# A decoder trunk in fp32: V and gate of four retention heads as two Strassen pairs woven into the memory and rotary passes

## The chip, the cores and the metric

The kernel runs on one core of one Trainium2 chip. The metric is device time in microseconds (us) of one execution. TensorE is PE in the profile (its weight loads are PEld), VectorE is DVE, ScalarE is ACT, GpSimd is POOL, SyncE is SP. PE, DVE, ACT, POOL and SP each work through their own queue in the order in which it was written when the kernel was compiled; a semaphore holds an instruction back until what it reads is there and what it overwrites is free.

## The reference, cut to what matters

256 tokens of width 2048 go through one layer A, a shared K/V projection, and one layer B. The part that is changed lies in layer A:

```python
h = rmsnorm(x, g)
q, k, v, gate_r, mq, gate_m = split_cols(h @ w_in, [1024, 1024, 2048, 2048, 1024, 1024])
q = rotary(q.reshape(B, S, 8, 128)); k = rotary(k.reshape(B, S, 8, 128)) * 128 ** -0.5
o = retention(q, k, v.reshape(B, S, 8, 256))          # 8 heads, chunks of 128 tokens
o = o * lax.rsqrt(jnp.mean(o * o, axis=-1, keepdims=True) + EPS)
o_ret = o.reshape(B, S, 2048) * jax.nn.silu(gate_r)
o_mem = memory_branch(mq, gate_m, mem_n, w_mem_kv)    # 4 heads of 256 over 256 memory tokens
return x + jnp.concatenate([o_ret, o_mem], axis=-1) @ w_out
```

`memory_branch` makes its keys and values as `mem_n @ w_mem_kv`, takes a softmax, and multiplies by a SiLU gate. After layer A, `shared_kv` projects the normed x to K and V of three groups of heads, and layer B uses them.

## The kernel before

Everything is fp32 in and out. A factor is split into a high part (a cast to fp32r, by ACT) and a low part (the difference, by DVE), and a product takes three matmuls: high with high, high with low, low with high. `split(hi, lo, src)` (L96 to L98) is these two instructions. A weight block is 128x1024: it comes by DMA into a `raw` tile (6 buffers), is split into `wh` and `wl` (5 buffers each), and PE consumes it. All weights are used once, so PE, ACT and DVE each have work for every block.

There are three forms of product:

- A **column pass** (`dense_cols`, L306) makes 512 output columns, transposed, in two halves. In each half it goes through 16 row groups of the weights and 2 column tiles, and for each it issues one matmul of 512 columns (L315, high and low part of x side by side) and one of 256 (L317): a pair. `cols_plain2`, `gate_cols` and `rotary` use it.
- A **row pass** (`dense`, L431) makes 256 tokens by 512 columns: 96 matmuls of 512 columns (L440 to L442). V and gate of the retention heads are made so.
- A **Strassen pair** (`strassen`, L343) makes two 512-column blocks at once with 7 products instead of 8. Each of its 4 depth steps loads 3 weight blocks, DVE makes sums and differences of them (L361), and 7 products of 6 matmuls each follow (L371 to L373). It needs differences of x as well (`combine`, L329, eight of them with their splits). It is a generator that is advanced a product at a time.

The order is fixed when the kernel is compiled. Small work (norms, splits of x, attention) is held in generators in `pending`; `step()` inside a pass advances one. A Strassen pair stands in `woven`; `weave(n)` in a column pass advances it n products, (2, 2, 1, 0) after the four parts of a half and 3 after its eviction. Splits and weight sums of a woven pair are put ahead with a priority, so the ACT and DVE queues have them earlier than PE's order would.

PSUM has three accumulators, acc0 to acc2, taken in turn, and two smaller tiles, att. While a pair is woven it holds two of the three (L345). SBUF has 30 tiles of 128x1024 named `big`, which hold x, its splits, results and attention operands. `spill` (L778) writes such a tile to DRAM and `fetch` (L784) reads it back, both on POOL's queue.

The stages of layer A, by the numbers of the profile: memory keys (`w_mk`) 5 to 56 us, memory values (`w_mv`) 56 to 101 us, then for each of two pairs of memory heads the queries and the gate (`w_ac`, L839 and L840), then for each of two groups of four heads rotary q and k (L844, L845) and for each pair of heads V and gate as row passes (L848, L849). Memory attention and retention are `pending` work that later passes step through (L841, L850). Retention ends in a power on POOL (L655). The out-projection, memory keys and values of layer B, and the K/V projection follow; the last, from 719 to 1203 us, weaves six Strassen pairs into column passes (L905 to L914). At the start x is read as `xs`, a `SplitCols`: ACT multiplies by the norm's gain and casts, DVE multiplies and subtracts (L220, L221). `Scaled` (L755), used behind layer A, has DVE scale a copy first and then split it.

## Time and profile before

| | us |
|---|---|
| median of 3 runs | 1902.02 |
| lowest and highest of them | 1897.88, 1902.39 |
| the profiled execution | 1899.93 |
| its span | 1898.2 |
| PE busy in it | 1875.5 |
| DVE busy in it | 1317.7 |
| ACT busy in it | 985.8 |

The span is the time from the first to the last instruction of the profiled execution; the execution's own time is 1.7 us longer. Busy times are sums over one engine. A row of waits gives the waiting engine and line, the engine and line it waited for, the total, the count and the longest. The lines are those of the kernel before; in the kernel after, the same code stands one or a few lines further down.

### The profile page before, as it was taken

To read this page: it belongs to the slowest core of one execution; us is meant where nothing else is said; L and a number is where in the kernel's file an instruction comes from. 1 tells how busy PE (TensorE), PEld (TensorE's weight loads), DVE (VectorE), ACT (ScalarE), POOL (GpSimd) and SP (SyncE) were. 2 spreads that over 40 slices of the span, in tenths; PEclk is the share of its full clock that TensorE was granted. 3 is DMA by queue.
4 is the path that set the end of the run, shared out by engine and by line. 5 is a ranking of instruction groups with operands and counts; after the bars stand their busy time and mean duration, and the time that the engine had idled before them with its cause. 6 is when DMAs were issued, how large, how long until landed. Compare 5 with 4: busy or idle time off the path is not lost.

```text
span 1898.2 us, 25963 instructions
## 1 busy us (share of the span) xinstructions
PE 1875.5 (99%) x9988; PEld 1604.6 (85%) x9988; DVE 1317.7 (69%) x1571; ACT 985.8 (52%) x1288; POOL 47.5 (3%) x88
## 2 busy tenths in 40 slices
PE   8999999999999999999999999999999999999997
PEld 7888888888888888888888888788889898888886
DVE  7766765665564757899999999866657475656643
ACT  6554445444454645555655556554545454545543
POOL 1000000000000000000000000000000000000000
PEclk9999999999999999999999999999999999999999
DMA  9654565565676666575766667666655556566462
GB/s 304 234 167 157 162 202 180 168 202 184 215 253 208 196 213 212 201 251 192 244 211 222 240 203 256 233 222 210 202 187 181 187 160 218 165 207 220 151 199 100
DMA packets 112588, 385.25 MB, mean 203 GB/s; under 512 B 12385, under 2 KB 18577, under 8 KB 112465
## 3 DMA queue, kind: packets, MB, share of 16 engines
q1 hardware_dynamic: 102784, 349.22, 56.5%
q0 software_dynamic: 9536, 34.37, 5.0%
q8 instruction: 78, 1.28, 0.3%
q14 instruction: 46, 0.37, 0.1%
q10 hardware_dynamic: 144, 0.01, 0.0%
HBM read 364.68 MB, written 18.87 MB: 202 GB/s over the span
## 4 chain that ended last, share of the span: by engine, by line
PE 93%; DVE 2%; issue 2%; ACT 1%; DMA 1%; SPq 0%; POOL 0%; ACTq 0%; POOLq 0%; DVEq 0%
PE acc L315 33%; PE acc L317 17%; PE acc L440 9%; PE acc L441 9%; PE acc L442 9%; PE acc L371 4%; PE acc L372 4%; PE acc L373 4%; DVE wl L98 1%; PE att L102 1%; PE att L103 1%; PE att L101 1%; PE acc L298 1%; ACT wh L97 1%; PE att L714 1%
## 5 line engine op out<-in xcount | busy, mean ns | idle before, releaser
L98 DVE TENSOR_TENSOR wl<-raw,wh 128x1024 fp32r<-128x1024 f32 (+1 forms) x642 | 769.3, 1209 | 461.8 <-ACT wh L97 459.9
L97 ACT CAST wh<-raw 128x1024 fp32r<-128x1024 f32 (+1 forms) x642 | 660.4, 1040 | 673.8 <-PE acc L315 263.6
L315 PE MATMUL acc<-big,wh 128*128 128x512 f32 x2752 | 983.5, 400 | 5.6 <-DVE big L221 2.4
L317 PE MATMUL acc<-big,wl 128*128 128x256 f32 x2752 | 771.3, 280 | 0.8 <-DVE wl L98 0.8
L315 PEld LDWEIGHTS acc<-big,wh 128*128 128x128 f32 x2752 | 517.8, 188 | 127.7 <-DVE big L470 3.1
L317 PEld LDWEIGHTS acc<-big,wl 128*128 128x128 f32 x2752 | 520.2, 189 | 5.0 <-DVE wl L98 1.1
L440 PE MATMUL acc<-wh,big 128*128 128x512 f32 x744 | 291.6, 392 | 0.0
L441 PE MATMUL acc<-wl,big 128*128 128x512 f32 x744 | 289.8, 390 | 0.0
L442 PE MATMUL acc<-wh,big 128*128 128x512 f32 x744 | 289.8, 390 | 0.0
L442 PEld LDWEIGHTS acc<-wh,big 128*128 128x128 f32 x744 | 139.7, 188 | 29.1
L440 PEld LDWEIGHTS acc<-wh,big 128*128 128x128 f32 x744 | 139.8, 188 | 28.2
L441 PEld LDWEIGHTS acc<-wl,big 128*128 128x128 f32 x744 | 139.8, 188 | 27.8
L371 PE MATMUL acc<-wh,big 128*128 128x512 f32 x336 | 133.2, 397 | 1.2 <-ACT wh L97 1.0
L372 PE MATMUL acc<-wl,big 128*128 128x512 f32 x336 | 131.7, 392 | 0.5 <-DVE wl L98 0.5
L373 PE MATMUL acc<-wh,big 128*128 128x512 f32 x336 | 131.6, 392 | 0.0
L97 ACT CAST wh<-big 128x1024 fp32r<-128x1024 f32 x72 | 75.5, 1049 | 72.5 <-DVE big L361 57.7
L98 DVE TENSOR_TENSOR wl<-big,wh 128x1024 fp32r<-128x1024 f32 x72 | 87.8, 1220 | 19.3 <-ACT wh L97 19.1
L371 PEld LDWEIGHTS acc<-wh,big 128*128 128x128 f32 x336 | 63.1, 188 | 17.1 <-ACT wh L97 1.7
L373 PEld LDWEIGHTS acc<-wh,big 128*128 128x128 f32 x336 | 63.1, 188 | 14.8
L372 PEld LDWEIGHTS acc<-wl,big 128*128 128x128 f32 x336 | 63.2, 188 | 11.8 <-DVE wl L98 1.0
L361 DVE TENSOR_TENSOR big<-big,raw 128x1024 f32<-128x1024 f32 x48 | 58.5, 1219 | 0.3
L98 DVE TENSOR_TENSOR big<-big 128x512 fp32r<-128x512 f32 (+1 forms) x54 | 43.4, 823 | 4.6 <-ACT big L97 3.2
(230 smaller groups left out, 1264.5 us busy)
## 6 DMA issues: line engine op xcount, KB each, us to landing
raw<-in_w_b_dram SPq DMA_DIRECT2D x160, 512.0 KB, 3.5
raw<-in_w_kc_dram SPq DMA_DIRECT2D x96, 512.0 KB, 4.4
raw<-in_w_vs_dram SPq DMA_DIRECT2D x96, 512.0 KB, 4.5
raw<-in_w_ac_dram SPq DMA_DIRECT2D x64, 512.0 KB, 3.5
raw<-in_w_ar_dram SPq DMA_DIRECT2D x64, 512.0 KB, 3.9
raw<-in_w_oa_dram SPq DMA_DIRECT2D x48, 512.0 KB, 3.5
raw<-in_w_ob_dram SPq DMA_DIRECT2D x48, 512.0 KB, 3.5
raw<-in_w_mv_dram SPq DMA_DIRECT2D x32, 512.0 KB, 3.5
```

Source lines behind the costliest of these rows:

```text
L97: act.copy(hi, src)
L98: dve.tensor_tensor(lo, src, hi.bitcast(F32), ALU.subtract)
L101: pe.matmul(o, lhsT=ah, rhs=bh, start=first, stop=False, skip_group_check=True)
L315: pe.matmul(ps[:, ct].rearrange("p h s -> p (h s)"), lhsT=wh[:, cs], rhs=xhl(part, a), start=first, stop=False, skip_group_check=True)
L317: pe.matmul(ps[:, ct, 0, :], lhsT=wl[:, cs], rhs=xh(part, a), start=False, stop=last, skip_group_check=True)
L361: f(*args)
L371: pe.matmul(ps, lhsT=h, rhs=wh[:, cs], start=first, stop=False, skip_group_check=True)
L372: pe.matmul(ps, lhsT=h, rhs=wl[:, cs], start=False, stop=False, skip_group_check=True)
L373: pe.matmul(ps, lhsT=l, rhs=wh[:, cs], start=False, stop=last, skip_group_check=True)
L440: pe.matmul(ps[t], lhsT=xh(part, a)[:, ts], rhs=wh, start=first, stop=False)
L441: pe.matmul(ps[t], lhsT=xh(part, a)[:, ts], rhs=wl, start=False, stop=False)
L442: pe.matmul(ps[t], lhsT=xl(part, a)[:, ts], rhs=wh, start=False, stop=last)
```

## The change

Layer A's V and gate of heads 0 to 3, four row passes, become two Strassen pairs (`w_as`), each giving V and gate of one pair of heads. Their products are advanced from inside the gate pass of the first memory pair, the query and gate passes of the second, and the rotary q pass of the first head group, at (2, 1, 1, 0) and 3. `xs` becomes a `Scaled` that scales in place (`own`), since the pairs need x times the gain for their differences. Memory keys and values of layer A are written to DRAM when they are made and fetched by `mem_job` when their attention begins; V and gate of the pairs are written by `done_a` and fetched by `ret_job`. Memory attention now runs in the rotary passes of the first head group, retention of heads 0 to 3 in those of the second. The first half of the second memory-key block takes the accumulator acc2 by name. In layer B, `mem_job` fetches and splits memory keys and values behind the gate pass instead of inside the query pass.

```diff
+    rate, banks = [2, 1, 1, 0, 3], []
-    def dense_cols(xs, w, c, evict, g=None):
+    def dense_cols(xs, w, c, evict, g=None, name=None):
         for i in range(2):
-            ps = acc_tile()
+            ps = acc_tile(name if i == 0 else None)
...
-                weave((2, 2, 1, 0)[j])
+                weave(rate[j])
...
-                weave(3)
+                weave(rate[4])
...
-    def strassen(parts, comb, w, done, banks=[]):
+    def strassen(parts, comb, w, done):
...
-            self.raw[j] = big_tile()
+            self.raw[j] = self.src[j] if self.own else big_tile()
...
+    def mem_job(mk, mv, q, gt, nrm, c):
+        k = split_big(fetch(mk))
+        yield
+        v = split_big_rows(fetch(mv))
+        yield
+        yield from mem_attention(q, k, v, gt, nrm, mix.tile(4 + c))
+
+    def ret_job(m, qT, kT):
+        v, gt = va[m]
+        v = split_big_rows(fetch(v))
+        gt = rows(fetch(gt))
+        yield
+        yield from retention(2 * m, 2 * (m % 2), qT, kT, v, gt, n_x.hr, mix.tile(m))
+        yield from mix.halves(m)
...
-    xs = SplitCols(xt, GA)
+    xs = Scaled(GA, own=True)
...
-        mk_a.append(split_big(mk0))
+        mk_a.append(spill(flat(mk0)))
...
-            yield from xs.halves(i)
+            yield from xs.start(i)
...
-    mk1 = cols_scaled(None, ms, w_mk[0], 1)
+    mk1 = cols_scaled(None, ms, w_mk[0], 1, name="acc2")
...
-    mk_a.append(split_big(mk1))
+    mk_a.append(spill(flat(mk1)))
...
-    mv_a = [rows_scaled2(dense(ms, w_mv[0], c), n_m.r) for c in range(2)]
+    mv_a = [spill(rows_scaled(dense(ms, w_mv[0], c), n_m.r).rearrange("p t c -> p (t c)")) for c in range(2)]
...
+    def done_a(m):
+        def f(o1, o2):
+            for t in range(2):
+                act.activation(o1[:, t, :], o1[:, t, :], AF.Copy, scale=n_x.r[:, t:t + 1])
+            g = gate_rows([o2[:, t, :] for t in range(2)], n_x.hr)
+            va[m] = [spill(o.rearrange("p t c -> p (t c)")) for o in (o1, g)]
+        return f
+
+    pending.append(combine(xs.raw, combx))
+    mq, gm = [], []
     for c in range(2):
-        mq = cols_plain2(xs, w_ac, 4 + c)
-        gm = gate_cols(n_x.bh, xs, w_ac, 6 + c)
-        pending.append(mem_attention(mq, mk_a[c], mv_a[c], gm, n_x, mix.tile(4 + c)))
-        pending.append(mix.halves(4 + c))
+        mq.append(cols_plain2(xs, w_ac, 4 + c))
+        if c == 0:
+            drain()
+            for m in range(2):
+                woven.append(strassen(xs, combx, w_as[m], done_a(m)))
+        gm.append(gate_cols(n_x.bh, xs, w_ac, 6 + c))
     for hg in range(2):
-        qT = rotary(cosr, sinr, xs, w_ac, hg)
-        kT = rotary(cosr, sinr, xs, w_ac, 2 + hg)
-        for u in range(2):
-            m = 2 * hg + u
-            v = rows_scaled2(dense(xs, w_ar, m), n_x.r)
-            gt = gate_rows(dense(xs, w_ar, 4 + m), n_x.hr)
-            pending.append(retention(2 * m, 2 * u, qT, kT, v, gt, n_x.hr, mix.tile(m)))
-            pending.append(mix.halves(m))
+        pending.append(mem_job(mk_a[hg], mv_a[hg], mq[hg], gm[hg], n_x, hg) if hg == 0 else ret_job(0, qT, kT))
+        q_ = rotary(cosr, sinr, xs, w_ac, hg)
+        pending.append(mem_job(mk_a[1], mv_a[1], mq[1], gm[1], n_x, 1) if hg == 0 else ret_job(1, qT, kT))
+        qT, kT = q_, rotary(cosr, sinr, xs, w_ac, 2 + hg)
+        if hg == 0:
+            while woven:
+                weave()
+    banks.clear()
+    for u in range(2):
+        m = 2 + u
+        v = rows_scaled2(dense(xs, w_ar, u), n_x.r)
+        gt = gate_rows(dense(xs, w_ar, 2 + u), n_x.hr)
+        if u == 0:
+            pending.append(mix.halves(4))
+            pending.append(mix.halves(5))
+        pending.append(retention(2 * m, 2 * u, qT, kT, v, gt, n_x.hr, mix.tile(m)))
+        pending.append(mix.halves(m))
...
+                rate[:] = [2, 2, 1, 0, 3]
...
-        pending.append(split_kv(c))
         mq = cols_plain2(yb, w_b, 16 + c)
         drain()
         gm = gate_cols(None, yb, w_b, 18 + c)
-        pending.append(mem_attention(mq, mkb2[c], mvb2[c], gm, n_y, mix.tile(4 + c)))
+        pending.append(mem_job(mk_b[c], mv_b[c], mq, gm, n_y, c))
```

Three places in the order of the engines' instructions. The first is PE's queue at the end of the first memory-key block and the start of the second; acc0_378 and acc2_378 are the accumulator of the second block's first half, acc1_112 the last one of the first block, and att_561 the tile of the norm's sums. Before:

```order
L298 MATMUL acc1_112<-big_322,wh_347 128x512
L300 MATMUL acc1_112<-big_322,wl_348 128x256
L174 MATMUL att_561<-ones_83,sqsum_395 128x1 x2
L315 MATMUL acc0_378<-big_126,wh_381 128x512
L317 MATMUL acc0_378<-big_126,wl_382 128x256
```

After:

```order
L299 MATMUL acc1_112<-big_322,wh_347 128x512
L301 MATMUL acc1_112<-big_322,wl_348 128x256
L316 MATMUL acc2_378<-big_126,wh_381 128x512
L318 MATMUL acc2_378<-big_126,wl_382 128x256
L316 MATMUL acc2_378<-big_126,wh_381 128x512
```

The second block's first matmul goes to acc2 instead of acc0, and the norm's sums no longer stand ahead of it.

The second is DVE's queue from the norm of x on, where the first column pass of layer A begins. `nbh` and `rope_t` are norm factors; `wl<-raw,wh` is a split of a weight block. Before, `big<-big,gain` is the low part of x:

```order
L201 TENSOR_SCALAR nsd_x<-r_x 128x2
L98 TENSOR_TENSOR wl<-raw,wh 128x1024
L521 SCALAR_TENSOR_TENSOR big<-acc_779,r_m,big 128x512
L198 TENSOR_SCALAR nbh<-nb 128x256
L810 TENSOR_TENSOR rope_t<-rope_t,nb 128x256
L811 TENSOR_TENSOR rope_t<-rope_t,nb 128x256
L221 SCALAR_TENSOR_TENSOR big<-big,gain 128x256
L521 SCALAR_TENSOR_TENSOR big<-acc_779,r_m,big 128x512
L221 SCALAR_TENSOR_TENSOR big<-big,gain 128x256 x2
L98 TENSOR_TENSOR wl<-raw,wh 128x1024
L221 SCALAR_TENSOR_TENSOR big<-big,gain 128x256 x8
L98 TENSOR_TENSOR wl<-raw,wh 128x1024
```

After, `big<-big 128x2x256` is the low part of x, L337 a difference of x and `big<-sm,big` or `big<-p,big` the low part of one:

```order
L202 TENSOR_SCALAR nsd_x<-r_x 128x2
L99 TENSOR_TENSOR wl<-raw,wh 128x1024
L337 TENSOR_TENSOR p<-big 128x512
L337 TENSOR_TENSOR p<-big,sm 128x512
L199 TENSOR_SCALAR nbh<-nb 128x256
L832 TENSOR_TENSOR rope_t<-rope_t,nb 128x256
L833 TENSOR_TENSOR rope_t<-rope_t,nb 128x256
L99 TENSOR_TENSOR big<-big 128x2x256 x7
L99 TENSOR_TENSOR wl<-raw,wh 128x1024
L99 TENSOR_TENSOR big<-big 128x2x256
L99 TENSOR_TENSOR big<-sm,big 128x512
L99 TENSOR_TENSOR wl<-raw,wh 128x1024
```

The eight differences and their splits now stand in this stretch, and x is split in eight instructions instead of sixteen.

The third is ACT's queue where the second pair ends. Before, this stretch of layer A is the row passes: weight casts, then V (L520) and gate (L527) from the accumulator:

```order
L97 CAST wh<-raw 128x1024 x6
L520 ACTIVATE big<-acc_2398,r_x 128x512
L97 CAST wh<-raw 128x1024
L520 ACTIVATE big<-acc_2398,r_x 128x512
L97 CAST wh<-raw 128x1024 x6
L527 ACTIVATE big<-acc_2549,hr_x 128x512
```

After, L528 is the tanh of the pair's gate, L867 the scaling of its V, the last `big<-big 128x1024` the cast of the fetched memory V of the second pair of heads, and L583 the exponentials of its attention:

```order
L528 ACTIVATE big<-big,hr_x 128x512
L98 CAST big<-p 128x512
L98 CAST big<-big 128x1024
L867 ACTIVATE big<-big,r_x 128x512
L428 COPY big<-acc_1279 128x512
L98 CAST wh<-raw 128x1024
L867 ACTIVATE big<-big,r_x 128x512
L98 CAST wh<-raw 128x1024 x2
L98 CAST big<-big 128x1024
L583 ACTIVATE p,ls<-acc_2915,nm,sc_x 128x256 x2
```

POOL's queue at that place, before:

```order
L184 TENSOR_TENSOR r_m<-r_m,mhalf 128x2
L184 TENSOR_TENSOR r_x<-r_x,mhalf 128x2
L655 TENSOR_TENSOR cf<-cf,mhalf 128x2 x8
L781 DMA spill_4620<-big 128x1024
L781 DMA spill_4847<-big 128x1024
```

And after, where 610, 614, 772 and 970 are memory K and V, 1997, 1995, 2859 and 2857 V and gate of the pairs:

```order
L783 DMA spill_1997<-big 128x1024
L783 DMA spill_1995<-big 128x1024
L808 DMA big<-spill_610 128x1024
L808 DMA big<-spill_772 128x1024
L808 DMA big<-spill_614 128x1024
L783 DMA spill_2859<-big 128x1024
L783 DMA spill_2857<-big 128x1024
L808 DMA big<-spill_970 128x1024
L808 DMA big<-spill_1995 128x1024
L808 DMA big<-spill_1997 128x1024
L656 TENSOR_TENSOR cf<-cf,mhalf 128x2 x2
```

The fetch of memory V of the second pair of heads (970) stands behind the spills of the second Strassen pair, and retention's powers stand behind all of these.

## Rows read from the trace of the kernel before

**Rows 1.** Page, part 1: busy us, share of the span, instructions

```profile
PE 1875.5 (99%) x9988; PEld 1604.6 (85%) x9988; DVE 1317.7 (69%) x1571; ACT 985.8 (52%) x1288; POOL 47.5 (3%) x88
```

**Rows 2.** PE's waits, whole run: line, releaser: total us, times, longest

```profile
PE acc L315 <- DVE big L221: 2.4, 1, 2.4
PE acc L315 <- DVE big L470: 2.2, 2, 2.0
```

**Rows 3.** Windows: us, busy PE, PEld, DVE, ACT, POOL, PEclk, DMA share, GB/s

```profile
300.00:460.00 160.00, 160.00 (x826) 136.52 (x825) 103.95 (x129) 79.66 (x112) 4.14 (x6) 1.00 0.57 184
745.00:840.00 95.00, 95.00 (x479) 79.98 (x478) 88.00 (x84) 53.50 (x57) 2.67 (x5) 1.00 0.68 224
745.00:1200.00 455.00, 453.22 (x2267) 380.01 (x2266) 425.04 (x400) 259.40 (x280) 11.19 (x21) 1.00 0.67 225
1240.00:1320.00 80.00, 80.00 (x474) 70.27 (x473) 49.31 (x58) 40.73 (x53) 2.16 (x4) 1.00 0.62 206
```

**Rows 4.** Waits from 100 to 460 us, layer A

```profile
ACT wh L97 <- PE acc L442: 55.6, 38, 1.7
```

**Rows 5.** Waits from 745 to 1190 us, the K/V weave

```profile
ACT wh L97 <- DVE raw L361: 83.1, 21, 6.2
ACT wh L97 <- DVE big L361: 55.1, 21, 4.2
...
ACT wh L97 <- PE acc L373: 12.4, 18, 3.1
```

**Rows 6.** Timeline, PE, row pass: start us, us, instruction

```profile
70.01 0.39 PE L442 MATMUL acc<-wh,big 128*128 128x512 f32 x1
...
70.69 0.39 PE L442 MATMUL acc<-wh,big 128*128 128x512 f32 x1
```

**Rows 7.** Timeline, PE, K/V weave: Strassen matmuls, then column pairs

```profile
769.85 0.39 PE L371 MATMUL acc<-wh,big 128*128 128x512 f32 x1
...
770.53 0.39 PE L315 MATMUL acc<-big,wh 128*128 128x512 f32 x1
...
772.64 0.40 PE L315 MATMUL acc<-big,wh 128*128 128x512 f32 x1
```

**Rows 8.** Timeline, PE, start of the second memory-key block, [idle before <-releaser]

```profile
30.93 0.50 PE L174 MATMUL att<-ones,sqsum 128*128 128x1 f32 x4
33.43 0.50 PE L315 MATMUL acc<-big,wh 128*128 128x512 f32 x1 [2.00 <-DVE big L470]
```

**Rows 9.** Timeline, PE, memory attention: first and last of 12 matmuls in a row

```profile
155.00 0.28 PE L101 MATMUL att<-big 128*128 128x256 f32 x1
...
156.32 0.28 PE L103 MATMUL att<-big 128*128 128x256 f32 x1
```

**Rows 10.** Timeline, DVE, K/V weave, instructions back to back

```profile
765.79 1.22 DVE L98 TENSOR_TENSOR wl<-big,wh 128x1024 fp32r<-128x1024 f32 x1
766.93 4.73 DVE L98 TENSOR_TENSOR wl<-raw,wh 128x1024 fp32r<-128x1024 f32 x4
...
788.13 0.68 DVE L405 TENSOR_TENSOR big<-acc,p 128x512 f32<-128x512 f32 x1
788.73 0.68 DVE L406 TENSOR_TENSOR big<-acc,p 128x512 f32<-128x512 f32 x1
```

**Rows 11.** DVE by form, 745 to 1190 us: busy, mean ns, idle before, releaser

```profile
L98 DVE TENSOR_TENSOR wl<-raw,wh 128x1024 fp32r<-128x1024 f32 x171 | 202.0, 1219 | 7.0 <-ACT wh L97 6.0
L98 DVE TENSOR_TENSOR wl<-big,wh 128x1024 fp32r<-128x1024 f32 x66 | 80.5, 1220 | 16.0 <-ACT wh L97 15.8
...
L361 DVE TENSOR_TENSOR raw<-raw 128x1024 f32<-128x1024 f32 x23 | 28.1, 1222 | 3.6 <-DMA raw<-in_w_vs_dram 3.2
...
L470 DVE TENSOR_TENSOR big<-acc,big 128x512 f32<-128x512 f32 x21 | 14.4, 684 | 1.2 <-ACT big L469 1.2
```

**Rows 12.** Instructions of the lines of spill (first) and fetch (second)

```profile
DMA to landing us min/median/max: 2.8/5.1/8.0
...
DMA to landing us min/median/max: 3.5/5.0/10.0
```

More of the change, by code (lines that the diff above doesn't have):

```diff
@@ L32, in yoco_trunk_kernel @@
     x, xt, memt,
-    w_ac, w_ar, w_oa, w_b, w_ob, w_mk, w_mv, w_kc, w_vs,
+    w_ac, w_ar, w_as, w_oa, w_b, w_ob, w_mk, w_mv, w_kc, w_vs,
     g_a, g_b, g_mem, g_kv, g_f,
@@ L489, in cols_plain2, with cols_scaled @@
         return h, l
-    def cols_scaled(b, *job):
+    def cols_scaled(b, *job, name=None):
         o = big_tile()
@@ L497, in evict @@
                 scale_half(o, i, b)
-        dense_cols(*job[:3], evict, *job[3:])
+        dense_cols(*job[:3], evict, *job[3:], name=name)
         return o
@@ L755, in yoco_trunk_kernel, with __init__ @@
     class Scaled:
-        def __init__(self, g):
+        def __init__(self, g, own=False):
+            self.own = own
             self.g, self.src, self.raw, self.parts, self.gens = g, {}, {}, {}, {}
@@ L782, in spill, with split_big_rows @@
         return d
+    def split_big_rows(o):
+        h, l = big_pair()
+        split(flat(h), flat(l), flat(o))
+        return rows(h), rows(l)
+    def mem_job(mk, mv, q, gt, nrm, c):
[11 more added lines that the diff above has]
+        yield from mix.halves(m)
     def fetch(d):
@@ L805, in stats_x @@
         for i in range(4):
-            yield from n_x.add(flat(xs.raw[i]))
+            yield from n_x.add(flat(xs.src[i]))
         yield from n_x.finish()
@@ L824, in yoco_trunk_kernel @@
         scale_half(mk1, i, n_m.b)
-    mk_a.append(split_big(mk1))
+    mk_a.append(spill(flat(mk1)))
     def load_x():
         for i in range(4):
-            xs.load(i)
+            xs.src[i] = big_tile()
+            sp.dma_start(out=xs.src[i], in_=xt[:, i])
             for _ in range(4):
@@ L833, in yoco_trunk_kernel @@
     pending.append(stats_x())
[L834 removed]
+    mv_a = [spill(rows_scaled(dense(ms, w_mv[0], c), n_m.r).rearrange("p t c -> p (t c)")) for c in range(2)]
     drain()
     mix = SplitMix()
[L838 to L851 removed]
+    combx, va = {}, {}
@@ L912, in yoco_trunk_kernel @@
                     woven.append(strassen(yk, comb, w_vs[p], done(p)))
+                rate[:] = [2, 2, 1, 0, 3]
     while woven:
         weave()
-    mkb2, mvb2 = {}, {}
-    def split_big_rows(o):
-        h, l = big_pair()
-        split(flat(h), flat(l), flat(o))
-        return rows(h), rows(l)
-    def split_kv(c):
-        mkb2[c] = split_big(fetch(mk_b[c]))
-        yield
-        mvb2[c] = split_big_rows(fetch(mv_b[c]))
-        yield
     for j in range(4):
@@ L1026, in _tables @@
     return rope, np.ascontiguousarray(decay), mask
-_ORDER = ["x", "xt", "memt", "w_ac", "w_ar", "w_oa", "w_b", "w_ob", "w_mk", "w_mv", "w_kc", "w_vs",
+_ORDER = ["x", "xt", "memt", "w_ac", "w_ar", "w_as", "w_oa", "w_b", "w_ob", "w_mk", "w_mv", "w_kc", "w_vs",
           "g_a", "g_b", "g_mem", "g_kv", "g_f", "rope", "decay", "mask"]
@@ L1072 @@
         "x": token_rows(xp), "xt": token_cols(xp), "memt": token_cols(mp),
-        "w_ac": cblocks(cat(w_in_a[0], (0, 2048), (6144, 8192))), "w_ar": rblocks(cat(w_in_a[0], (2048, 6144))),
+        "w_ac": cblocks(cat(w_in_a[0], (0, 2048), (6144, 8192))), "w_ar": rblocks(cat(w_in_a[0], (3072, 4096), (5120, 6144))),
+        "w_as": sblocks(cat(w_in_a[0], (2048, 2560), (4096, 4608), (2560, 3072), (4608, 5120))),
         "w_oa": rblocks(w_out_a[0]), "w_b": cblocks(w_in_b[0]), "w_ob": rblocks(w_out_b[0]),
```

## The prediction

> **What bounds the kernel now.** I read the totals first: TensorE (PE) is busy for 1875.5 of the 1898.2 us, VectorE (DVE) for 1317.7 and ScalarE (ACT) for 985.8 [rows 1]. Busy PE time is modelled, so I read PE's own waits next [rows 2]: the longest are 2.4 us once and 2.2 us in two, and the whole list comes to about 14 us. So every column pass that PE no longer does is time won, as long as DVE and ACT still deliver on time. How near DVE is to failing differs by stage [rows 3]. At 300 to 460 us in layer A, where nothing is woven, DVE works 104 of 160 us. At 745 to 1200 us, where the six Strassen pairs of the shared K/V are woven into column passes, it works 425 of 455 us. Who waits for whom turns round too. In the plain stretch ACT's weight casts wait for PE to give back a buffer, 55.6 us for the row passes alone: the splits run ahead [rows 4]. In the woven stretch the same casts wait for DVE's sums of weight blocks, 83.1 and 55.1 us, and for PE's products only 12.4 us [rows 5]. PE and DVE are level there, with a cover of little.
>
> **PE: the work removed.** The V and gate blocks of heads 0 to 3 were four row passes of 96 matmuls, 384 in all. Two Strassen pairs have 7 products x 4 x 6 = 168 each, 336 in all. All move 512 columns. In a row pass three starts lie 0.68 us apart [rows 6], in the woven stretch three starts too, 0.68 us [rows 7]: 0.227 us each in either form. So 48 x 0.227 = **-10.9 us**.
>
> **PE: the bank.** PE waits 2.0 us at 33.4 us [rows 8]: the second memory-key block begins in the bank that the first has just filled, and DVE is still emptying it. The order shows it now starting in acc2. Its first weights are not late: in this trace the rows before end at 30.9 us and only the bank's eviction is named. So **-2.0 us**, at worst 0. The other early wait, 2.4 us for the split of x [rows 2], stays: between the spread of the norm and the first half of x, the queue still has the rope scaling and now two differences of x that belong to the mixing. I leave it at 2.4.
>
> **DVE: the work added, against the work it must keep up with.** Take the stretch that the woven part spans, from the first half of x to the end of the second pair. By the order, PE has there 352 column pairs (512 and 256 columns), 336 Strassen products and 84 attention instructions. A pair takes 2.11 / 6 = 0.352 us [rows 7], an attention matmul 1.32 / 11 = 0.12 us [rows 9]; the 12 transposes, of half the columns, I put at 0.11. PE needs 123.9 + 76.3 + 8.6 + 1.3 = 210.1 us. DVE has 229 instructions: 137 of 128x1024 (105 splits and 32 sums), 73 of 512 elements and 19 small ones. Back to back a 128x1024 starts 1.14 us after the last, and a 512 one 0.60 [rows 10]: 156.6 + 44.5 + about 6 (19 small ones at 0.3, half a 512 one) = 207.1 us. That is 98.6% of PE's need, where the woven stretch of before shows 425/455 = 93.4% [rows 3].
>
> DVE cannot run without gaps in this form: after a sum it waits until ACT has cast it, so that it can subtract. Those waits are measured [rows 11]: 16.0 us before the 66 splits of sums, which makes 5.8 us for the 24 in two pairs. The splits of plain weights have 7.0 us for 171, so up to 3.3 us for the 81 here; some of that is PE holding buffers and goes when DVE is late, so 0 to 3.3. The first sums wait for loads 3.6 us in 23, 1.3 us for 8; evictions 1.2 us in 21, in this stretch about 60 such instructions, 2 to 3 us. I take 11 us, between 9 and 13. Then DVE needs 218.1 us where PE needs 210.1: **+8.0 us** of PE waiting. Bounds: the very first part alone gives the least. From the first half of x to the seventh weight block of the first pair DVE has 35 instructions, 14 x 1.14 + 21 x 0.60 = 28.6 us (the eight mixing differences and their splits stand there too), and PE has 64 pairs and 19 products, 26.8 us: 1.8 us are lost whatever follows. The most: the window with the most idle beside its work, 7.0 us in 95 [rows 3], gives 8% or 16.5 us, and a loss of 13.5.
>
> The Trainium skill has a rule that speaks against the change (VectorE: DVE Perf Modes, section "The TRN2 errata"): a two-input fp32 operation costs a fixed 151 cycles beside its elements. By it a 128x1024 is 1.22 us and a 512 one 0.69, an estimate that matches the durations of the rows (1.22 and 0.68 [rows 10]); used as the queue's pace it would give 137 x 1.22 + 73 x 0.69 + 6 = 224 us before any wait, and a loss of 25 us. The starts, 1.14 and 0.60 us apart [rows 10], show that 0.08 us of each lies under its neighbour, so I don't use it.
>
> **The round trip through DRAM.** Memory K and V of both pairs of heads, and V and gate of the two Strassen pairs, are spilled and fetched: eight writes and eight reads on POOL's queue. A spill lands after 5.1 us and a fetch after 5.0 (3.5 to 10.0) [rows 12]. The casts that split K and V twice are not new, they are moved from the start into the woven stretch and counted above. Seven of the eight fetches stand far ahead of their use. The eighth is memory V of the second pair: on POOL it stands behind the spill of the second pair's V, which waits for ACT's scaling at the pair's end. ACT's own queue has two casts between that scaling and the cast of the fetched tile, so ACT, with its weight casts and exponentials queued behind, stands about 0.5 + 5.0 - 2 x 1.0 = 3.5 us; DVE's split of the same tile stands behind it, and PE's transposes wait for the exponentials. Part of it lies under what DVE has in hand: **+1.0 us**, from 0 to 8.5 (landing at 10.0). POOL's powers for retention stand behind these fetches as well, but they are due some 30 us later.
>
> **The K/V weave's entrance, and layer B.** The order puts the mixing of layer B a little closer together; nothing in the trace shows the price. I bound it with 0 and 1 and take **+0.5 us**. In layer B the fetches of memory K and V and their splits go from the memory-query pass into the pass behind it: the same instructions, under a stretch where DVE works 49 of 80 us and PE never stands in the row from 1240 of [rows 3], so **0**; without that cover one landing, 5 us.
>
> **Sum.** -10.9 - 2.0 + 8.0 + 1.0 + 0.5 = -3.4 us. The profiled execution took 1899.93 us, so 1896.5; the median of the runs, 1902.02, is 2.1 above it, so **1898.6 us** on the median. The ends: least loss, -10.9 - 2.0 + 1.8 = -11.1, 1890.9 us; most, -12.9 + 13.5 + 8.5 + 1 = +10.1, 1912 us. A measurement of this kernel tells about 0.3%, 5.7 us, from no change: faster than 1896.3, slower than 1907.7.
>
> **The rivals.**
> - *DVE keeps pace.* In the K/V weave PE waited only about 2 of 455 us for its operands (453.2 busy [rows 3]). If layer A's does as well after its first 1.8 us, the time is 1902.0 - 11.1 = 1891 us. For it: the waits of DVE for ACT shrink when neither is held by PE, and ACT has over 40% free. Against it: DVE's work is 98.6% of PE's instead of some 93%, and ACT's waits [rows 5] say that even there the buffers had run dry.
> - *The late fetch sets the end: slower.* If the fetch of memory V lands at 10 us and ACT, then DVE, then PE stand for it while DVE has no time in hand, the 8.5 us come on top of a loss near its upper end: -12.9 + 12 + 8.5 + 0.5 = +8, 1910 us. It decides from a landing of about 8 us on, or from DVE idle of 10% of its work. For it: PE, ACT and DVE all stand in order, and DVE has 1.4% free. Against: the median landing is half of that.
> - *The pace is a whole duration.* The rule above, from rows: 1.22 and 0.68 us for each instruction, nothing overlapped, loss 25 us, -12.9 + 25 + 1.5 = +13.6, 1916 us. The starts in [rows 10] exclude it as long as the queue is not broken up by waits.
>
> **How the numbers follow.** The forecast, DVE setting the pace with 5 to 12 us lost, has 0.57 (of that 0.14 is faster by over 0.3%, 0.41 within, 0.02 slower); DVE keeping pace 0.28 (0.24 faster, 0.04 within); the late fetch 0.13 (0.04 within, 0.09 slower); the whole duration 0.02 (slower). Together 0.38 faster, 0.49 within 0.3%, 0.13 slower. The range is from the first rival's 1891 to 1907: what it leaves out is the slower cases and a part of the first.
>
> **What would show it.** PE's waits named for the split of weights between 100 and 320 us: 5 to 12 us in all if I am right, under 3 if DVE keeps pace; a first cluster right at the first products. DVE over 93% busy there. ACT idle before the cast of a fetched tile near 310 us: 2 to 5 us, or more for the second rival. No wait for the bank near 31 us. Matmuls of row form 48 x 8 = 384 fewer, Strassen ones 336 more. If PE's waits are small and the time is still near 1902, the products' own pace is what I have wrong.

## The result and the profile after

The change makes the kernel slower: 1927.02 us median of 4 runs (1925.32 to 1927.92) against 1901.58 us of 4 runs before (1897.88 to 1902.39). The ratio is 1.0137, with a 95% interval from 1.0119 to 1.0154. The forecast was 1898.6 us within 1891 to 1907, so the time lies outside the range, on the side that the prediction had given 0.13.

The totals of the change's page, its part 1, to be read against [rows 1]:

```profile
PE 1881.3 (98%) x9940; PEld 1603.1 (83%) x9940; DVE 1396.9 (73%) x1663; ACT 1014.3 (53%) x1322; POOL 55.3 (3%) x104
```

PE has 48 matmuls fewer and is busy for 5.8 us longer. Either it works slower somewhere, or the page counts time as busy in which it does little. PE's own waits name where it stands (line, releaser: total us, times, longest), to be read against [rows 2]:

```profile
PE acc L372 <- ACT wh L98: 11.7, 7, 3.7
PE acc L373 <- DVE wl L99: 5.0, 7, 1.9
PE att L595 <- DVE p L589: 3.9, 1, 3.9
PE acc L299 <- ACT wh L98: 3.0, 1, 3.0
PE acc L316 <- DVE big L99: 2.6, 1, 2.6
PE acc L372 <- DVE big L362: 2.2, 1, 2.2
```

L372 and L373 are Strassen products; L99 is the low part of a split, L98 the cast, L362 a weight sum. The 2.2 us of the bank are gone from the list. The 3.0 us at L299 are the first weights, at 11.6 us: the first three runs below, with the same code there, wait 0.4 to 0.7 us on that line, so some 2 us at the start of this trace are not the change's doing.

To see how much each stage lost I set the same weight split, counted from the end of the program, beside itself in both traces. The change is 24.9 us late when layer A's row passes end, 4.6 us more behind the first products of the K/V weave (24.9 at the 380th split from the end, 29.5 at the 360th), 2.9 us less behind the entrance of layer B, and 26.9 us at the end. Nearly everything is lost in layer A. There, from the first column pass to the end of the row passes of V and gate, the 336 products in place of the 384 row matmuls save 10.9 us at the row passes' own pace of 0.228 us, and 21.3 us more are standing than before. The rest, some 15 us, are matmuls that start farther apart than before without a wait between them; about 10 of these, an estimate from the starts, lie in the stretches of the lower clock shown next.

Windows of the change show both (columns as in [rows 3]; the fifth overlaps its neighbours):

```profile
140.00:145.00 5.00, 5.00 (x30) 4.32 (x29) 0.00 (x0) 0.00 (x0) 0.00 (x0) 1.00 0.02 10
145.00:150.00 5.00, 2.21 (x13) 1.65 (x11) 2.14 (x3) 0.87 (x2) 0.00 (x0) 1.00 0.00 0
150.00:155.00 5.00, 2.29 (x5) 1.68 (x6) 5.00 (x6) 5.00 (x6) 0.00 (x0) 0.69 0.06 20
155.00:160.00 5.00, 5.00 (x15) 3.88 (x14) 4.97 (x5) 0.07 (x1) 0.00 (x0) 0.62 0.91 299
152.00:158.00 6.00, 4.79 (x11) 3.79 (x12) 6.00 (x7) 3.07 (x4) 0.00 (x0) 0.50 0.47 140
...
340.00:345.00 5.00, 1.05 (x7) 0.68 (x6) 2.06 (x6) 3.14 (x7) 0.00 (x0) 0.81 1.03 420
345.00:350.00 5.00, 4.01 (x15) 3.12 (x14) 4.64 (x8) 2.01 (x6) 0.00 (x0) 0.50 0.91 339
350.00:355.00 5.00, 5.00 (x26) 4.53 (x25) 3.22 (x5) 1.21 (x2) 0.00 (x0) 0.67 0.10 37
```

From 140 to 145 us PE works and DVE, which was said to be the bound, does nothing at all. From 147 to 153 us PE stands but for a few matmuls, and from 148 us DVE is full. Then PE is "busy" for all of 155 to 160 us with 15 matmuls instead of some 27: the granted clock is 0.62 there in the mean, and 0.50 from 152 to 158 us. DVE's queue in that place (start us, duration us, instruction, [idle before <-releaser]):

```profile
136.69 1.22 DVE L362 TENSOR_TENSOR big<-raw 128x1024 f32<-128x1024 f32 x1
147.86 0.69 DVE L471 TENSOR_TENSOR big<-acc,big 128x512 f32<-128x512 f32 x1 [9.95 <-ACT big L470]
148.47 1.22 DVE L362 TENSOR_TENSOR raw<-raw 128x1024 f32<-128x1024 f32 x1
149.60 0.69 DVE L539 TENSOR_TENSOR big<-big,nbh 128x512 f32<-128x512 f32 x1
150.20 1.22 DVE L362 TENSOR_TENSOR big<-big,raw 128x1024 f32<-128x1024 f32 x1
151.34 0.68 DVE L542 SCALAR_TENSOR_TENSOR big<-sm,big 128x512 f32<-128x512 f32 x1
151.94 1.22 DVE L99 TENSOR_TENSOR wl<-raw,wh 128x1024 fp32r<-128x1024 f32 x1
```

ACT's queue at the same place, with the eviction's copy and then the cast of the second sum:

```profile
147.24 0.58 ACT L470 COPY big<-acc 128x512 f32<-128x512 f32 x1 [11.54 <-PE acc L318]
149.72 1.04 ACT L98 CAST wh<-raw 128x1024 fp32r<-128x1024 f32 x1 [1.89 <-DVE raw L362]
```

And PE's queue, with the products that need those sums:

```profile
150.81 0.51 PE L372 MATMUL acc<-wh,big 128*128 128x512 f32 x1 [3.61 <-ACT wh L98]
153.21 0.79 PE L373 MATMUL acc<-wl,big 128*128 128x512 f32 x1 [1.89 <-DVE wl L99]
153.80 0.63 PE L374 MATMUL acc<-wh,big 128*128 128x512 f32 x1
154.23 0.63 PE L372 MATMUL acc<-wh,big 128*128 128x512 f32 x1
...
159.09 0.40 PE L372 MATMUL acc<-wh,big 128*128 128x512 f32 x1
159.32 0.40 PE L373 MATMUL acc<-wl,big 128*128 128x512 f32 x1
```

The gate pass's half, which PE finishes at 147.2 us, is evicted by ACT's copy (L470) and DVE's fold (L471). The fold stands between the first and the second of the three weight sums of the next depth step. So DVE, ten microseconds ahead, waits for PE (through ACT's copy, which is named as the releaser and itself waited 11.54 us for PE); when PE is through, the products it wants next need sums that could not be made; PE waits 3.6 and 1.9 us for fold, sums, cast and split one after the other, with two steps of the gate (L539, L542) between them. The queues of ACT and DVE are strictly in order, says the Trainium skill (PSUM — Partial Sum Buffer, section "Engine vs sequencer instructions"); the 9.95 us in front of L471, with sums behind it, are what that looks like. Behind the stand the matmuls start 0.43 us apart instead of 0.23, until 159 us: the lower of the two clock levels, 1.2 GHz. The same picture stands at 243 to 254 us, where the second pair's first depth step ends.

### The profile page after: what moved, and what is told of

It is laid out like the page before. It is cut to its first block, busy times and chain, and to the rows that moved or that the text cites. A ratio compares the mean times of both kernels' runs of the same rounds, so it can differ in the third digit from the quotient of the medians.

```text
span 1925.1 us, 26067 instructions
## 1 busy us (share of the span) xinstructions
PE 1881.3 (98%) x9940; PEld 1603.1 (83%) x9940; DVE 1396.9 (73%) x1663; ACT 1014.3 (53%) x1322; POOL 55.3 (3%) x104
## 4 chain that ended last, share of the span: by engine, by line
PE 88%; DVE 6%; issue 3%; DMA 1%; ACT 1%; POOL 0%; SPq 0%; ACTq 0%; POOLq 0%; DVEq 0%
PE acc L316 31%; PE acc L318 15%; PE acc L441 7%; PE acc L442 7%; PE acc L443 7%; PE acc L373 5%; PE acc L374 4%; PE acc L372 4%; DVE wl L99 3%; ACT wh L98 1%; DVE big L362 1%; PE acc L299 1%; PE att L103 1%; PE att L102 1%; PE att L104 1%
## 5 line engine op out<-in xcount | busy, mean ns | idle before, releaser
L99 DVE TENSOR_TENSOR wl<-raw,wh 128x1024 fp32r<-128x1024 f32 (+1 forms) x642 | 766.5, 1209 | 379.9 <-ACT wh L98 377.8
L98 ACT CAST wh<-raw 128x1024 fp32r<-128x1024 f32 (+1 forms) x642 | 658.1, 1039 | 591.9 <-PE acc L316 224.0
L372 PE MATMUL acc<-wh,big 128*128 128x512 f32 x448 | 180.1, 402 | 14.1 <-ACT wh L98 11.7
L373 PE MATMUL acc<-wl,big 128*128 128x512 f32 x448 | 178.7, 399 | 5.1 <-DVE wl L99 5.0
L98 ACT CAST wh<-big 128x1024 fp32r<-128x1024 f32 x96 | 100.7, 1049 | 107.9 <-DVE big L362 89.7
L99 DVE TENSOR_TENSOR wl<-big,wh 128x1024 fp32r<-128x1024 f32 x96 | 117.2, 1221 | 29.4 <-ACT wh L98 29.1
L372 PEld LDWEIGHTS acc<-wh,big 128*128 128x128 f32 x448 | 85.1, 190 | 37.1 <-ACT wh L98 16.5
L373 PEld LDWEIGHTS acc<-wl,big 128*128 128x128 f32 x448 | 85.6, 191 | 23.1 <-DVE wl L99 8.4
L362 DVE TENSOR_TENSOR big<-big,raw 128x1024 f32<-128x1024 f32 x64 | 78.0, 1220 | 0.4
L99 DVE TENSOR_TENSOR big<-big 128x512 fp32r<-128x512 f32 (+1 forms) x66 | 53.3, 831 | 7.5 <-ACT big L98 6.0
```

The costliest lines, as they stand in the source:

```text
L98: act.copy(hi, src)
L99: dve.tensor_tensor(lo, src, hi.bitcast(F32), ALU.subtract)
L362: f(*args)
L372: pe.matmul(ps, lhsT=h, rhs=wh[:, cs], start=first, stop=False, skip_group_check=True)
L373: pe.matmul(ps, lhsT=h, rhs=wl[:, cs], start=False, stop=False, skip_group_check=True)
```

## What the experiments told apart

Times are medians. Kernels that ran side by side share the runs of the kernel before: 1900.56 us for the first four below, then 1899.99 for four, 1899.65 for three and 1900.93 for the last two. A ratio is to these, with its 95% interval. The change itself ran beside 1901.58 us, so a gain against its 1927.02 us is a difference between two sets of runs: by the ratios the gains below are 25.7, 18.1 and 9.1 us where the medians give 25.5, 18.3 and 7.9.

**Where the sums stand.** The first run moves one product per half from behind the eviction to ahead of it; a depth step has four products, so its next sums are needed, and queued, earlier.

```diff
-    rate, banks = [2, 1, 1, 0, 3], []
+    rate, banks = [2, 2, 1, 0, 2], []
```

> The change with one edit: products of the pairs advanced at (2, 2, 1, 0) and 2 instead of (2, 1, 1, 0) and 3, seven per half as before, the same instructions on every engine. Theory (order): PE's two long stalls, at 147 to 153 us and 243 to 249 us of the change's trace, come from the second and third weight sum of a depth step standing on DVE behind the eviction of the half that PE is still computing. With five products ahead of the eviction these sums are in DVE's queue early, both stalls go (5.5 and 4.8 us of standing) and so does the half clock behind each (about 2.7 us each): 1927 - 16 = about 1911 us. Rival (pace): DVE has 98.6% of PE's need as work, so the same idle time comes up at other places: 1923 us or more, and PE's waits between 125 and 310 us still sum to about 14 us.

1901.5 us, ratio 1.0002 (0.9992 to 1.0011): 25.5 us gained, more than the order theory wanted. Both stands are gone, and so is the one at 344 us. The next run keeps the rate and moves only the sums and their loads:

```diff
+        nxt = sums(0)
+        for d in range(4):
+            w11, w12, w22, s1 = nxt if early or d == 0 else sums(d)
...
             product(b3, w11, own(0, 0), d, f, l)
+            if early and not l:
+                nxt = sums(d + 1)
...
```

> The change with PE's order kept as it is: only the loads and the three weight sums of the next depth step are written one product earlier, so that they stand ahead of the eviction on DVE. Theory (order): both long stalls go, as with the other interleaving, about 1911 us. Rival (pace): no more than 4 us gained, 1923 us or more. If only the interleaving on PE mattered and not DVE's queue, this run stays at 1927 us.

1908.7 us, ratio 1.0042 (1.0028 to 1.0057): 18.3 us gained against 16 expected. Both stands are gone here too; the longest waits left before 310 us are 2.6 us at the first column pass, as in the change, and 2.2 us at 217 us. DVE's idle time in front of the same fold is down to 0.94 us (this run's timeline of DVE):

```profile
145.44 0.69 DVE L479 TENSOR_TENSOR big<-acc,big 128x512 f32<-128x512 f32 x1 [0.94 <-ACT big L478]
```

PE's work and DVE's work are what they were (9940 matmuls, 1396.3 us of DVE against 1396.9); what moved is the place of the sums on DVE and of their loads. Late loads are no rival: at both stands of the change the sum that PE wanted stood behind the fold and waited for no load. The pace theory, as a cause of these stands, falls.

**The late fetch.** The stand at 344 us begins at 334 us on POOL (the change's timeline of POOL):

```profile
333.51 0.54 POOL L783 DMA_DIRECT2D spill<-big  x1 [1.40 <-ACT big L867]
334.04 1.58 POOL L808 DMA_DIRECT2D big<-spill  x3
```

ACT's cast of what was fetched:

```profile
341.86 1.04 ACT L98 CAST big<-big 128x1024 fp32r<-128x1024 f32 x1 [5.61 <-DMA big<-spill]
```

PE's transposes of that attention:

```profile
344.69 1.11 PE L595 MATMUL att<-ident,p 128*128 128x128 f32 x4 [3.95 <-DVE p L589]
```

The fetch of memory V is issued right behind the spill of the second pair's V and is used 7.8 us later; ACT stands 5.6 us of that with its weight casts behind it, then PE stands, then PE runs at a granted clock of 0.50 (the window from 345 us above).

```diff
-        k = split_big(fetch(mk))
+        k, v = fetch(mk), fetch(mv)
+        k = split_big(k)
         yield
-        v = split_big_rows(fetch(mv))
+        v = split_big_rows(v)
```

> The change with memory V fetched together with memory K, when memory attention of a pair of heads begins. Theory (late fetch): ACT's 5.6 us wait for the landing at 342 us, PE's stand of 4.0 and 1.0 us at 344 and 347 us and the half clock behind it (about 4 us) go: 1927 - 8 = about 1918 us; the rest of the waits stays. Rival (cover): DVE has been busy without a break up to that place, so the wait moves to its splits and no more than 3 us are gained, 1924 us.

1919.15 us, ratio 1.0089 (1.0073 to 1.0105): 7.9 us gained, near the 9 of the late-fetch theory; in the trace layer A ends 7.2 us earlier than in the change. Together with the 18.3 us of the sums that makes 26.2, about the 25.5 us of the first run. There the fetch is as late, 308.4 us for a cast at 316.0, but ACT's order has one weight cast more ahead of the cast of V, these wait for PE anyway, and ACT does not stand for the landing.

**The bank and the turn of the accumulators.** Outside a weave, passes take acc0 and acc1 in turn; inside one every half takes acc0 (the words "in turn" for all three, ahead of the prediction, were too coarse).

```diff
...
-    mk1 = cols_scaled(None, ms, w_mk[0], 1)
+    mk1 = cols_scaled(None, ms, w_mk[0], 1, name="acc2")
```

> The kernel before with one edit: the first half of the second memory-key block takes accumulator acc2. Theory: PE's wait of 2.0 us at 33.4 us goes and nothing takes its place, 1901.6 - 2.0 = 1899.6 us, and the start of x in layer A is 2 us earlier. Rival: the first weights or the norm of the memory tokens are late instead, and the time stays within 0.5 us of 1901.6.

1898.4 us, ratio 0.9984 (0.9975 to 0.9994): 2.2 us gained by the medians, 3.0 by the ratio. But the trace has more in it: this kernel, which has nothing else of the change, also stands at the K/V weave's entrance and also gains at layer B's. A half that takes acc2 by name does not move the turn, so every later pass has the other accumulator. At the K/V weave the last unwoven half then has acc0, which the first woven half needs. In the kernel before PE goes straight on with column pairs until 746.8 us:

```profile
746.70 0.28 PE L317 MATMUL acc<-big,wl 128*128 128x256 f32 x1
746.81 0.49 PE L371 MATMUL acc<-wh,big 128*128 128x512 f32 x1
```

In the change four products come first, all of a depth step's (PE, first and last of their 24 matmuls):

```profile
767.50 0.40 PE L372 MATMUL acc<-wh,big 128*128 128x512 f32 x1
...
773.32 0.40 PE L374 MATMUL acc<-wh,big 128*128 128x512 f32 x1
```

So PE wants the next step's sums at 773.7 us, and the order puts two splits ahead of the second of them (the change's timeline of DVE):

```profile
769.86 1.22 DVE L362 TENSOR_TENSOR big<-raw 128x1024 f32<-128x1024 f32 x1
770.99 2.35 DVE L99 TENSOR_TENSOR wl<-raw,wh 128x1024 fp32r<-128x1024 f32 x2
773.26 1.22 DVE L362 TENSOR_TENSOR raw<-raw 128x1024 f32<-128x1024 f32 x1
```

PE, where it needs them:

```profile
775.69 0.51 PE L372 MATMUL acc<-wh,big 128*128 128x512 f32 x1 [1.98 <-ACT wh L98]
776.37 0.59 PE L316 MATMUL acc<-big,wh 128*128 128x512 f32 x1 [0.17 <-DVE big L471]
776.75 0.41 PE L318 MATMUL acc<-big,wl 128*128 128x256 f32 x1
776.96 0.63 PE L316 MATMUL acc<-big,wh 128*128 128x512 f32 x1
```

In the run with the bank edit alone PE waits as long at the same place (timeline, PE):

```profile
746.77 0.49 PE L371 MATMUL acc<-wh,big 128*128 128x512 f32 x1 [1.98 <-ACT wh L97]
```

Two runs put the turn back (the first pair of added lines); the second of them also moves it on ahead of layer B (the last added line):

```diff
             ps = acc_tile(name if i == 0 else None)
+            if name and i == 0:
+                turns["acc"] += 1
...
+    turns["acc"] += 1
     for j in range(4):
         pending.append(yb.start(j))
```

> The kernel before with acc2 for the first half of the second memory-key block, as in the bank run, but the turn of acc0 and acc1 is counted on as if the half had taken its own, so that every later pass has the accumulator that it has in the kernel before. Theory (turn): the 2.0 us stand at the K/V weave's entrance (4.6 us with the half clock behind it) and the 2.9 us gained at layer B's entrance are both due to the swapped accumulators, not to anything else in the change: 1898.4 - 4.6 + 2.9 = 1896.7 us, with no wait of PE over 1 us between 740 and 760 us, and the wait of 1.1 us at about 1224 us back. Rival (shift in time): they come from all work starting 2 us earlier, and the time stays at 1898.4 us with the stand at about 747 us.

> The same, with the turn of acc0 and acc1 moved on by one again just ahead of layer B. Theory (turn): the K/V weave's entrance as in the kernel before, layer B's entrance as in the change: 1898.4 - 4.6 = 1893.8 us. Rival (shift in time): no difference to the bank run, 1898.4 us.

1894.74 us (0.9970, 0.9959 to 0.9982) and 1894.75 us (0.9971, 0.9960 to 0.9982). In both, the stand at the K/V entrance is gone. In the first the wait at layer B's entrance is back, at 1224.05 us with 1.06 us, as in the kernel before; in the second it is gone. The traces decide for the turn, at both places: from one side of the K/V entrance to the other the bank run loses 4.6 us against the kernel before, these two lose nothing. The times show it less well: by the ratios they are 2.7 and 2.5 us under the bank run, where 1.7 and 4.6 were expected, and the difference between the two is under what such runs resolve. Either of the two kernels is faster than the kernel before by 0.3%, with none of the Strassen work in layer A.

**What the two pairs bring once the order is right.** The next run has the first run's rate and takes away the 32 weight sums of layer A's pairs:

```diff
-            s1, s2 = flat(big_tile()), flat(big_tile())
-            ahead(dve.tensor_tensor, s1, w11, w12, ALU.add)
-            ahead(dve.tensor_tensor, w12, w12, w22, ALU.add)
-            ahead(dve.tensor_tensor, s2, s1, w22, ALU.add)
+            s1, s2 = w11, None
...
+            s2 = w21 if s2 is None else s2
```

> The change with products advanced at (2, 2, 1, 0) and 2, and in layer A the 32 weight sums of the pairs left out: the products take the plain blocks, with as many casts, splits, loads and matmuls as before. Theory (pace): what is left of the loss there (5 us of PE standing in the weave, some 3 behind it, some 5 of lower clock and small gaps) is DVE's pace, and with 32 x 1.14 = 36.5 us less to do on DVE most of it goes: 1901.5 - 8 = about 1893 us. Rival (evictions): PE stands because each woven half has to use acc0, and DVE's folds stand behind casts; then no more than 2 us go, 1899.5 us.

These products no longer compute V and gate; the run serves for the time alone. 1895.5 us, ratio 0.9974 (0.9962 to 0.9985), 6.0 us less than the first run, which has the sums, of 8 expected (5.3 by the ratios; in the traces 5.5 at the end of layer A). Windows from 125 to 300 us, of the change, of the first run and without the sums:

```profile
125.00:300.00 175.00, 160.38 (x785) 132.48 (x784) 148.06 (x150) 94.68 (x112) 2.67 (x5) 0.96 0.54 184
```

```profile
125.00:300.00 175.00, 170.69 (x878) 142.92 (x878) 162.89 (x169) 103.15 (x124) 2.68 (x5) 1.00 0.59 202
```

```profile
125.00:300.00 175.00, 174.96 (x905) 147.24 (x904) 135.59 (x145) 110.65 (x128) 3.10 (x6) 1.00 0.61 205
```

With DVE at 163 of 175 us PE lacks 4.3 us; at 136 it lacks nothing. That is DVE's work in the way, but it does not say whether by its amount, by its order, or by the wait of a cast for a sum, which goes too. And it shows that even with no loss in the weave the pairs bring only 2 us against the bank run between the first column pass and the out-projection. The starts of PE's matmuls say where the rest of the 10.9 us goes. In a weave a triple of products takes 0.697 us, with the changes between passes and products in it, in this run and in the kernel before's K/V weave alike, where [rows 7] had shown 0.68 within one product: 1.5 us. The first pairs run at a lower clock in this run, 0.74 from 100 to 105 us: 1.4 us by its starts. The bank run's trace has 1.00 there and the kernel before's 0.50 from 105 to 108 us, so that part is not the pairs' doing. Behind the weave, memory attention and retention share the rotary passes: 3.6 us of standing in the change's own stages and some 3 us of slower pairs and attention.

All corrections together, with the sums in:

```diff
-    rate, banks = [2, 1, 1, 0, 3], []
+    rate, banks = [2, 2, 1, 0, 2], []
...
+            if name and i == 0:
+                turns["acc"] += 1
...
+            if early and not l:
+                nxt = sums(d + 1)
...
+        k, v = fetch(mk), fetch(mv)
...
+    turns["acc"] += 1
     for j in range(4):
```

> The change with products advanced at (2, 2, 1, 0) and 2, sums of the next depth step written one product earlier, memory V fetched with memory K, the turn of acc0 and acc1 as in the kernel before up to the K/V weave and moved on by one ahead of layer B. By the order theory and the turn theory: 1901.5 - 4.6 = 1896.9 us, less about 2 us for the sums that are earlier, 1895 us. Rival (pace): the waits in layer A move and nothing is gained there, 1897 us; if the turn has no part in it, 1900 us or more.

1895.2 us, ratio 0.9971 (0.9960 to 0.9983), as expected, and no better than the two kernels without the pairs. Spreading the pairs over more passes was to give DVE time. Three runs do so, all with the fetch and the turn as above. The first has (2, 1, 1, 0) and 1 with the sums early, the second (1, 1, 1, 0) and 2 with the sums early, the third (2, 1, 1, 0) and 1 with the sums where the change has them; the pairs may run on to the rotary q pass of the second head group:

```diff
-    rate, banks = [2, 1, 1, 0, 3], []
+    rate, banks = [2, 1, 1, 0, 1], []
...
         qT, kT = q_, rotary(cosr, sinr, xs, w_ac, 2 + hg)
-        if hg == 0:
-            while woven:
-                weave()
...
         q_ = rotary(cosr, sinr, xs, w_ac, hg)
+        if hg == 1:
+            while woven:
+                weave()
```

> The change with its two pairs spread thinner: products advanced at (2, 1, 1, 0) and 1, five per half instead of seven, so that the second pair ends in the rotary q pass of the second head group; sums of the next depth step written one product earlier, memory V fetched with memory K, the turn of the accumulators as in the last run (kernel before's up to the K/V weave, moved on by one ahead of layer B). Theory (pace): with the same DVE work over some 40% more column matmuls the stands in the weave go (5.1 us with seven per half), and with them the lower pace behind them: 1895 - 5 = about 1890 us. Rival (the two streams): PE loses time wherever column pairs and pair products take turns, whatever DVE does, and memory attention and retention now run beside a woven pair: 1895 us or more.

> As the run above with (1, 1, 1, 0) and 2, also five per half, so that the fourth product of the first depth step stands behind the eviction instead of ahead of it. Theory (pace): as above, about 1890 us, since the sums are early either way. Theory (order): where the eviction stands between a depth step and its sums the stand comes back for one or two halves, 3 to 6 us more than the run above.

> As the first of the three, (2, 1, 1, 0) and 1, but with the sums where the change has them. The first depth step of each pair again ends just ahead of an eviction, as in the change. Theory (order): the stand behind that eviction is back once per pair, about 5 us each with a half clock behind it: 8 to 16 us more than with the sums early. Rival (pace): DVE has time in hand at five per half, so at most 2 us more.

1900.05 us (1.0003, 0.9993 to 1.0013), 1906.25 us (1.0030, 1.0018 to 1.0041) and 1907.16 us (1.0040, 1.0025 to 1.0055). The first was a miss of 10 us: thinner is not faster. DVE works 156 of 175 us in the same window, less than above, and PE stands more (windows and PE timeline of the first):

```profile
125.00:300.00 175.00, 169.92 (x889) 142.51 (x888) 156.28 (x164) 102.38 (x121) 3.69 (x7) 0.99 0.61 206
```

```profile
269.39 0.49 PE L374 MATMUL acc<-wh,big 128*128 128x512 f32 x1 [2.39 <-ACT wh L98]
```

The sums before that product stand on DVE behind rotary's and attention's steps, one of which waits for a cast. The third is 7.1 us slower than the first, less than the 8 to 16 of the order theory and well above the 2 of pace: by the starts of the column matmuls it is 7.7 us behind from the weave on, where PE stands 3.6 us at 146 and 3.4 us at 277 us. The second's 6.2 us (3 to 6 expected) look like order too, but they are not. Its column matmuls are level with the first's within 1.4 us at 371 us and 6.0 us behind at 387: another fetch, issued at 373.0 us, is late there. ACT, where it casts what was fetched, and then PE:

```profile
379.77 1.05 ACT L98 CAST big<-big 128x1024 fp32r<-128x1024 f32 x1 [7.07 <-DMA big<-spill]
```

```profile
385.72 0.46 PE L102 MATMUL att<-big,ph 128*128 128x256 f32 x1 [3.97 <-ACT ph L98]
```

So order still counts at five products per half, as the third run shows, and thinning alone does not take away what remains; how much of it is DVE's amount stays open.

Two last runs tried the two places that were left, on top of all corrections: retention of heads 0 to 3 moved into the row passes, and then also the second pair's first sums ahead of the first pair's end.

```diff
...
         m = 2 + u
+        if u == 0:
+            pending.append(ret_job(0, q0, k0))
+            pending.append(ret_job(1, q0, k0))
         v = rows_scaled2(dense(xs, w_ar, u), n_x.r)
...
+            if l and then is not None:
+                first[then[0]] = sums(0, then[1], ks), ks
...
```

> The run with all corrections and seven products per half (1895.2 us), with one more edit: retention of heads 0 to 3 is stepped through in the row passes of V and gate behind the rotary passes, as such work was in the kernel before, not in the rotary passes themselves. Theory (sharing): behind the weave PE stands 2 to 4 us and its column pairs are slower by some 2 us because DVE and ACT serve rotary and retention in the same passes; with retention in the row passes 3 to 4 us go, about 1891.5 us. Rival: these stands belong to the retention of the heads itself (its powers, fetches and transposes wait for each other wherever it is put), and the time stays within 1.5 us of 1895.

> As the run above, and the first three weight sums of the second pair are written ahead of the last three products of the first pair. Theory (order): the stand at the change of pairs (about 1.0, 0.5 and 0.5 us near 215 us) goes, 1.5 to 2 us less than the run above. Rival (pace): DVE has nothing in hand there and the stand moves behind the change of pairs, no difference.

1895.9 us (0.9970, 0.9958 to 0.9982) and 1894.7 us (0.9970, 0.9959 to 0.9981): the rival in both. The stands move with retention (0.5, 0.5 and 0.7 us in the row passes) and, at the change of pairs, from the first product (1.0, 0.4 and 0.5 us) to the pass behind it (0.2 and 1.5 us).

## Why the prediction was wrong, step by step

- **Products, -10.9 us.** Number and pace were right within a pass: 48 matmuls fewer at 0.228 us. The changes between passes and products take 1.5 us of it; the row that was read [rows 7] had none in it.
- **Bank, -2.0 us.** Right in size: 2.2 us, 3.0 by the ratio. What the name does to the turn of the other two accumulators was not seen, though the diff shows it: a pass that takes a named tile does not count.
- **DVE's work, +8.0 us. This is the step that failed.** It set the sum of DVE's work in the whole stretch against the sum of PE's. (With 1.14 and 0.60 us as printed that sum is 206.0 and not 207.1 us; nothing hangs on it.) A sum holds only if the queue never waits for the engine that waits for it. Here it did: DVE idle for 9.95 and 4.69 us, then PE standing 5.5 and 4.6 us, at the two places where a depth step ends just ahead of an eviction. The order of instructions was at hand: in the change's DVE queue the fold of the gate's half stands between two sums, and PE's next instructions need both. The prediction counted those instructions instead of reading them across the two engines. Its own sign says so: DVE was to be over 93% busy, and in the change it worked 148 of the 175 us from 125 to 300, 85%, while PE's waits for casts and splits up to 310 us came to 12.7 us. With the order mended, PE waited 5.1 us in the weave and 1901.5 us came out, near the forecast's 1898.6 for pace alone; but by the thinner runs that number is not shown to be DVE's amount either, and the agreement may be luck.
- **What a stand costs.** Every term priced a stand at its own length. The trace puts a stretch at half clock behind the long ones: from 153.2 to 158.9 us thirteen matmuls took 5.6 us in place of 3.0, and likewise at 249 and 345 us. In the whole of layer A matmuls that started farther apart, without a wait, made some 15 us, about 10 of them at the lower clock. No term, no rival and no end of the range had it.
- **Round trip, +1.0 us, at most 8.5.** Measured 7.9, the half clock behind the stand included. The rival had mechanism, place and size: fetch behind the spill, ACT, DVE and PE in a row, from a landing of 8 us on (7.8 measured). The median landing of [rows 12] was taken although the row's maximum was 10.0 and three fetches and two spills stand together here; and the cover that was hoped for was not there: DVE was busy for 23.8 of the 25 us from 310 to 335.
- **K/V weave's entrance, +0.5 us.** 4.6 us, by the turn of the accumulators and the clock behind a 2.0 us stand (3.2 us in the run without sums, where the same stand had no lower clock behind it). **Layer B, 0 us:** 2.9 us gained, also by the turn; the new place of the fetches, which I had thought to be the only edit there, does not show: the bank run, without it, gains the same.
- **Rivals and range.** The whole-duration rival (1916 us) gave the nearest time, for a reason that plays no part: starts of DVE back to back are 1.14 us apart in the change too. The range ended at 1907 since the order was never a case of its own.

## What to carry to other kernels

Before work is woven into another stream, follow one eviction through all queues: whatever stands behind an instruction that waits for PE must not be what PE needs next. A balance of busy times says nothing on that, and moving the weave by one product in seven was worth 25 us here, more than the change could have won. Count a PE stand with the clock behind it, and after an edit to which accumulator is taken, look at every later place where the turn decides.

## What the runs showed of the hardware that was not expected

The granted clock fell to the lower level behind stands of 5.5 us (at 147 us, two waits), 4.6 us (243 us) and 4.0 us (341 us), and also behind shorter ones: 2.6 us at 103 us and 2.0 us at 774 us, where column pairs of 0.35 us took 0.59. It did not behind 2.2 us at 226 us, where the windows from 225 to 235 us show 1.00. Nor is it the place: the run with the sums early has that same 2.2 us stand, at 217 us, with the lower clock behind it, and the run without sums has the 2.0 us stand of the K/V entrance, at 745 us, without it (windows of the two):

```profile
219.00:222.00 3.00, 3.00 (x9) 2.33 (x8) 3.00 (x4) 2.53 (x3) 0.55 (x1) 0.50 0.79 208
```

```profile
745.00:750.00 5.00, 4.82 (x26) 3.98 (x26) 3.06 (x4) 1.74 (x2) 0.53 (x1) 1.00 0.87 299
```

The Trainium skill (TensorE: Matmul & The Clock Gate, section "What's actually happening") says that the clock follows how busy the engine has just been and has these two levels only. The rows agree, and these short stands show that neither the length of a wait nor the instructions around it tell alone. What tells them apart was not tried.
